# Forgetting attention by pairs of query blocks, with merged transposes and values ordered behind projections

## The chip, the cores and the metric

One core of a Trainium2 chip runs the whole kernel. The metric is the time of one execution on the device, in microseconds (us). The engines are TensorE (PE), VectorE (DVE), ScalarE (ACT), GpSimd (POOL) and SyncE (SP); each takes its own instructions in the order in which they stand in its queue. Here SP mainly issues DMAs, all transposes among them.

## The reference

A decoder trunk of two layers on 2048 tokens of 1024 channels. The even layer runs eight heads of forgetting attention (FoX) and four heads of gated linear attention (GLA) from one input projection; the odd layer runs retention and dilated attention. The change is about FoX, and about transposes that both layers share:

```python
def forgetting_attention(q, k, v, logf):
    c = jnp.cumsum(logf, axis=-1)
    ...
    def one_block(args):                       # 128 queries
        i, qi, ci = args
        s = jnp.einsum('bhqd,bhkd->bhqk', qi, k) * scale
        s = s + ci[..., :, None] - c[..., None, :]
        s = jnp.where(kpos[None, :] <= qpos[:, None], s, -jnp.inf)
        p = jax.nn.softmax(s, axis=-1)
        return jnp.einsum('bhqk,bhkd->bhqd', p, v)

def even_layer(h, norm_g, w_in, b_f, w_lr, b_lr, gla_g, w_out):
    u = rmsnorm(h, norm_g)
    z = u @ w_in
    ...                                        # FoX heads o_a, GLA heads o_b
    mix = jnp.concatenate([merge_heads(o_a), o_b], axis=-1)
    return h + (mix * jax.nn.silu(gate)) @ w_out
```

## The kernel before

Every float32 operand of a product is held as two fp16 parts, so a projection is three matmuls per tile (L163 to L165 with tokens on the rows, L173 to L175 with tokens on the columns). put_u makes the normed stream: for each of 16 row tiles it takes the sum of squares into a tile of its own (junk), splits the tile into u_hi and u_lo, and transposes each by a DMA of its own (L103) into uh and ul.

FoX goes head by head. tiles projects q, k and v of the next head, two row tiles at a time, and transposes the columns in three DMAs for every four row tiles (L413). For a query block i, scores computes the products with the keys of blocks 0 to i (L498, L499), adds the causal mask (L501), takes scores plus decay out of PSUM with their maximum in one DVE instruction per 1024 columns (L502), takes the exponential (L508), splits it into fp16 parts fx_ph (ACT, L511) and fx_pl (DVE, L512), and has SP transpose both, into fx_th (L515) and fx_tl (L516). values multiplies them with v (L524, L525) and scales the result (L526, L527, ACT L529, DVE L534); after four blocks POOL stores it to mix_d (L538).

A head's 16 blocks come in the order 12, 0, 13, 1, 14, 2, 15, 3, 8, 4, 9, 5, 10, 6, 11, 7. Each of fx_ph, fx_pl, fx_th and fx_tl has one buffer for the small blocks (under 8) and one for the large. The values of a block are emitted two steps behind its scores. merge spreads the projections for the next head (Heads.units) and those that go to memory (Extra: the gate's factors and the GLA operands, stored by POOL) evenly over these steps. Then the compile-time scheduler, with a model of time of its own, sets each engine's queue: what was emitted is where it starts from, not the order that results.

After head 6 no next head is left; the last head is merged with what is left of Extra (SHARE1), with loads of the output weights and with the first GLA rows; a rest of Extra (left, L1076) follows it. Then mix_out goes over 16 row tiles: load, gate, split into u_hi and u_lo, two transposes (yh, yl), the products, the residual, and put_u for the odd layer.

Of the kernel before, what the change touches and what calls it, by code (L numbers as in the profile page):

```python
# [29 lines left out]
SHARE2, REST2 = 80.0, 40.0  # L30
LAG = 2  # steps from scores to values
LAG_EVEN, LAG_ODD = 2, 2  # row tiles from the output's operands to its products


class Core:
    """Tools that both layers share: norms, weights in two fp16 parts, products."""

    def __init__(self, ctx, tc, cst):
# [13 lines left out]
        self.pending = None  # L52
# [8 lines left out]
    def pow2_scale(self, s, inv, ssq):  # L61
        """Powers of two s and inv = 1 / s with sqrt(ssq) * s < 2**14.5."""
# [7 lines left out]
    def rstd(self, ssq, n, shift, k=1):  # L70
        """2**shift / sqrt(ssq / n + EPS)"""
# [44 lines left out]
    def start_w(self, w, segs, gain, pool=None, space=None):  # L116
        """Columns of a weight times the gain of their rows, in two fp16 parts, and the scale's inverse."""
# [37 lines left out]
    def rows(self, out, u, t, w, c0, c1):  # L155
        """out[token, column] = u[tile t] @ w[:, c0:c1]"""
        nc = self.nc
        b, j = divmod(t, 4)
        uh, ul = u[b]
        wh, wl = w[0], w[1]  # L160
        for k in range(KT):
# [31 lines left out]
def take(units, cost):  # L193
    """The first units that come to about a cost, taken off their list."""
# [7 lines left out]
class Extra:  # L202
    """Products that go to memory: silu's two factors, and the operands of the recurrent heads."""
# [16 lines left out]
    def rows(self, n, t, k, store):  # L220
        """Row tiles t and t + 1 of 256 columns."""
# [13 lines left out]
    def cols(self, n, b, c, k, store):  # L235
        """128 columns of a block of 512 tokens."""
# [41 lines left out]
class Recurrent:  # L278
    """The steps of recurrent heads in their order, and the rows that they made."""
# [11 lines left out]
def mix_out(co, work, inputs, h_d, gate_d, gate_k, kept_d, first, ws, recur, finish, lag):  # L291
    """h + (mix * silu(gate)) @ w_out by row tiles; mix is kept_d, from column 512 * first, next to the recurrent
# [908 lines left out]
```

## Time and profile before

| what | value |
|---|---|
| three runs | 2424.91, 2433.67 (median), 2436.22 us |
| span of the profiled execution | 2434.8 us |
| PE busy | 2208.3 us (91%), clock 0.955 on the mean |
| DVE, ACT, POOL busy | 1579.2 (65%), 1166.1 (48%), 493.0 us (20%) |
| packets of transposes and stores, queue q1 | 57.2% of 16 DMA engines |

For the profiled execution only the span is recorded; it lies between the median run and the slowest one. PE is the busiest engine, so a microsecond counts where PE stands idle or has a lower clock. In the page's 40 slices of 61 us PE is at 5 to 8 tenths in the first five (up to 300 us), mostly at 8 or 9 up to about 910 us, and mostly at 9 after that. FoX runs from 170 to 1040 us, mix_out of the even layer follows to about 1310 us, then the odd layer.

### The profile page before, as it was taken

What the parts mean: (1) busy time and instruction counts of PE and PEld (TensorE: products, weight loads), DVE (VectorE), ACT (ScalarE), POOL (GpSimd) and SP (SyncE); (2) the same over time, 40 slices, a digit from 0 to 9 for tenths busy, and PEclk for the clock granted to TensorE, in tenths of its full rate; (3) what the DMA queues carried; (4) which work ended last, traced back from release to release, by engine and by line L of the source; (5) the groups of instructions that cost most, each with busy time, mean ns of one, the idle gap of its engine ahead of it and who ended that gap; (6) DMA issues with size and microseconds to landing.
All of it is one profiled execution on the core that took longest, in us unless ns stands there. A gap on an engine that the chain in (4) does not pass through costs nothing.

```text
span 2434.8 us, 52412 instructions
## 1 busy us (share of the span) xinstructions
PE 2208.3 (91%) x19956; PEld 1701.8 (70%) x19956; DVE 1579.2 (65%) x5190; ACT 1166.1 (48%) x2772; POOL 493.0 (20%) x510
## 2 busy tenths in 40 slices
PE   5877889798898899999999999999899899899998
PEld 4766768565667788764447888788787787765554
DVE  5456656765657567766557676666675666687774
ACT  5534445444545445544444555455453445633322
POOL 1020111101011111111111231222212122145341
PEclk8899889899999999999999999999999999989999
DMA  9868877878878686898876777885867768866653
GB/s 229 164 123 138 144 134 139 153 133 138 154 127 161 127 151 141 172 258 202 220 194 148 138 148 144 145 177 114 160 123 151 136 130 150 164 220 173 178 173 104
DMA packets 846652, 381.95 MB, mean 157 GB/s; under 512 B 749232, under 2 KB 805440, under 8 KB 846144
## 3 DMA queue, kind: packets, MB, share of 16 engines
q1 hardware_dynamic: 748976, 259.31, 57.2%
q0 software_dynamic: 23584, 82.33, 12.3%
q10 hardware_dynamic: 73840, 36.97, 6.5%
q8 instruction: 156, 2.56, 0.5%
q14 instruction: 96, 0.79, 0.1%
HBM read 135.40 MB, written 73.73 MB: 86 GB/s over the span
## 4 chain that ended last, share of the span: by engine, by line
PE 58%; DMA 22%; DVE 10%; issue 4%; ACT 3%; SPq 2%; POOL 1%; ACTq 0%; POOLq 0%; DVEq 0%
PE dn L163 10%; PE dn L165 10%; PE dn L164 10%; DMA fx_tl<-fx_pl 7%; PE dn L334 3%; PE dn L336 3%; PE dn L335 3%; DMA dl_pt<-dl_pl 3%; PE big L873 2%; PE big L874 2%; DMA w_raw<-in_w_in_even_dram 2%; PE aux L524 2%; PE big L498 2%; DMA fx_th<-fx_ph 1%; PE big L499 1%
## 5 line engine op out<-in xcount | busy, mean ns | idle before, releaser
L163 PE MATMUL dn<-w,uh 128*128 128x192 f16 (+1 forms) x3840 | 1012.2, 264 | 13.1 <-DVE head L407 6.7
L165 PE MATMUL dn<-w,ul 128*128 128x192 f16 (+1 forms) x3840 | 1011.1, 263 | 8.1 <-DMA ul<-u_lo 8.1
L164 PE MATMUL dn<-w,uh 128*128 128x192 f16 (+1 forms) x3840 | 1011.9, 264 | 0.0
L163 PEld LDWEIGHTS <-uh 128*128 128x128 f16 x3968 | 394.7, 100 | 51.6 <-DMA uh<-u_hi 10.9
L165 PEld LDWEIGHTS <-ul 128*128 128x128 f16 x3968 | 393.3, 100 | 42.0 <-DMA ul<-u_lo 14.4
L164 PEld LDWEIGHTS <-uh 128*128 128x128 f16 x3968 | 394.0, 100 | 32.2 <-issue 4.0
L508 ACT ACTIVATE fx_s<-fx_s,fx_nm 128x1664 f32<-128x1664 f32 (+15 forms) x128 | 153.4, 1199 | 163.0 <-DVE fx_nm L507 154.2
L880 ACT ACTIVATE dl_s<-dl_s,dl_m 128x256 f32<-128x256 f32 (+1 forms) x384 | 172.7, 452 | 114.9 <-DVE dl_m L879 99.4
L512 DVE TENSOR_TENSOR fx_pl<-fx_s,fx_ph 128x1664 f16<-128x1664 f32 (+15 forms) x128 | 165.9, 1298 | 92.4 <-ACT fx_ph L511 55.2
L876 DVE CUSTOM_DVE_ANT_0 dl_s<-big,dl_mask,hd_f 128x256 f32<-128x256 f32 (+1 forms) x384 | 141.8, 421 | 58.2 <-PE big L874 57.1
L502 DVE CUSTOM_DVE_ANT_0 fx_s<-big,cb,hd_f 128x1024 f32<-128x1024 f32 (+7 forms) x128 | 133.6, 1046 | 49.6 <-PE big L501 26.5
L511 ACT ACTIVATE fx_ph<-fx_s 128x1664 f16<-128x1664 f32 (+15 forms) x128 | 141.0, 1106 | 51.3 <-DMA fx_th<-fx_ph 45.3
L524 PE MATMUL aux<-head,fx_th 128*128 128x128 f16 x1088 | 125.8, 229 | 43.0 <-DMA fx_th<-fx_ph 41.4
L525 PE MATMUL aux<-head,fx_tl 128*128 128x64 f16 x1088 | 114.6, 201 | 45.9 <-DMA fx_tl<-fx_pl 45.7
L77 POOL TENSOR_TENSOR rs_r<-rs_v,mhalf 128x1 f32<-128x1 f32 (+2 forms) x96 | 71.1, 743 | 389.0 <-DVE rs_v L74 354.9
L883 DVE TENSOR_TENSOR dl_pl<-dl_s,dl_ph 128x512 f16<-128x512 f32 (+2 forms) x96 | 100.4, 1048 | 69.6 <-ACT dl_ph L882 38.8
L524 PEld LDWEIGHTS <-fx_th 128*128 128x128 f16 x1088 | 103.1, 104 | 54.4 <-DMA fx_th<-fx_ph 49.4
L525 PEld LDWEIGHTS <-fx_tl 128*128 128x128 f16 x1088 | 98.3, 102 | 56.7 <-DMA fx_tl<-fx_pl 54.6
L83 DVE SCALAR_TENSOR_TENSOR w<-w_raw,w_gs,w 128x256 f16<-128x256 f32 (+2 forms) x296 | 123.3, 466 | 11.0 <-ACT w L82 10.9
L873 PE MATMUL big<-head 128*128 128x256 f16 (+1 forms) x384 | 129.5, 355 | 0.6 <-DVE dl_rec L876 0.6
L874 PE MATMUL big<-head 128*128 128x256 f16 (+1 forms) x384 | 129.7, 357 | 0.0
L498 PE MATMUL big<-head 128*128 128x512 f16 (+3 forms) x320 | 114.1, 357 | 15.3 <-DVE fx_m L502 13.6
(235 smaller groups left out, 4340.1 us busy)
## 6 DMA issues: line engine op xcount, KB each, us to landing
gate_d<-x_out POOLq DMA_DIRECT2D x64, 256.0 KB, 4.0
o_gate<-gate_d SPq DMA_DIRECT2D x32, 512.0 KB, 4.6
rec_d<-dl_rec POOLq DMA_DIRECT2D x16, 528.0 KB, 5.3
dl_rec<-rec_d POOLq DMA_DIRECT2D x16, 528.0 KB, 6.2
x_h<-in_x_dram SPq DMA_DIRECT2D x16, 512.0 KB, 4.7
cb<-cum_d SPq DMA_DIRECT2D x16, 512.0 KB, 9.5
o_mix<-mix_d SPq DMA_DIRECT2D x32, 256.0 KB, 3.2
o_h<-in_x_dram SPq DMA_DIRECT2D x16, 512.0 KB, 4.6
```

The costliest lines, as they stand in the source:

```text
L163: nc.tensor.matmul(out, uh[:, k, xs], wh[:, k, c0:c1], start=k == 0, stop=False)
L164: nc.tensor.matmul(out, uh[:, k, xs], wl[:, k, c0:c1], start=False, stop=False)
L165: nc.tensor.matmul(out, ul[:, k, xs], wh[:, k, c0:c1], start=False, stop=k == KT - 1)
L498: nc.tensor.matmul(p[:, k0:k1], q, st[:, 1, ks], start=True, stop=False)
L508: nc.scalar.activation(raw[:, :n], raw[:, :n], AF.Exp, bias=nm[:, 0:1], accum_out=nm[:, 1:2])
L512: nc.vector.tensor_sub(pl[:, :n], raw[:, :n], ph[:, :n])
L524: nc.tensor.matmul(pv, th[:, k, :], v[:, k, :], start=k == 0, stop=False)
L525: nc.tensor.matmul(pv[:, 0:64], tl[:, k, :], v[:, k, 0:64], start=False, stop=k == i)
L873: nc.tensor.matmul(p[:, sp], st[:, 0, qs], st[:, 1, ks], start=True, stop=False)
L874: nc.tensor.matmul(p[:, sp], st[:, 0, qs], st[:, 2, ks], start=False, stop=True)
L876: nc.vector.tensor_tensor_reduce(out=raw[:, sp], in0=p[:, sp], in1=mask[:, 256 - 128 * len(vs):], scale=f[:, 0:1], scalar=-3.0e38, op0=OP. ...
L880: nc.scalar.activation(raw[:, sp], raw[:, sp], AF.Exp, bias=m[:, i:i + 1], accum_out=rec[:, n, 65:66])
```

## The change

Blocks go in pairs. Pair n is the blocks 15 - n and n, always 17 tiles of 128 keys (W is 17 * 128), so that a head has eight steps of one size. One copy, one subtraction, two transposes, one reciprocal and one multiplication serve both blocks; the exponential stays one per block. The scores of a pair lie in fx_s, one buffer in work for even n and one in the weights' pool for odd n (from start_gla on only the first), and the subtraction writes its fp16 result in place, into the front half of fx_s. fx_ph, fx_th and fx_tl have two buffers each. The result is scaled by one DVE instruction of 128 x 256 (o2), and two POOL additions join the parts; ACT's part of that is gone.

values is called by behind, which orders it after the last projection matmul emitted so far (co.last). periods puts LEAD1 = 4 units of Extra first in each head's period, and the last head's extra work comes in at every second place instead of every fifth. The transposes of put_u (u_x into ut), of mix_out (u_x into yt) and of q and k in the even layer (chunked, three into one) are merged; put_u's squares go to the half of u_x that later takes the low part, in place of junk.

```diff
@@ put_u
-        junk = work.tile([128, D], BF16, name="junk", bufs=1)
+        x = work.tile([128, 2, D], F16, name="u_x", bufs=U_BUFS)
         ssq = self.small.tile([128, 1], F32, name="ssq")
-        nc.scalar.activation(junk, h, AF.Square, accum_out=ssq)
-        hi = work.tile([128, D], F16, name="u_hi", bufs=U_BUFS)
-        lo = work.tile([128, D], F16, name="u_lo", bufs=U_BUFS)
+        nc.scalar.activation(x[:, 1].bitcast(BF16), h, AF.Square, accum_out=ssq)
         r = self.rstd(ssq, D, 10)
-        self.split(hi, lo, h, r[:, 0:1])
-        for part, x in zip(u[b], (hi, lo)):
-            nc.sync.dma_start_transpose(part[:, :, j * 128:(j + 1) * 128], x)
+        self.split(x[:, 0], x[:, 1], h, r[:, 0:1])
+        nc.sync.dma_start_transpose(u[b].rearrange("p s k n -> p (s k) n")[:, :, j * 128:(j + 1) * 128],
+                                    x.rearrange("p s n -> p (s n)"))
@@ mix_out
-        nc.sync.dma_start_transpose(yh, hi)
-        nc.sync.dma_start_transpose(yl, lo)
+        yt = work.tile([128, 2, KT, 128], F16, name="yt", bufs=lag + 1)
+        nc.sync.dma_start_transpose(yt.rearrange("p s k n -> p (s k) n"), x.rearrange("p s n -> p (s n)"))
@@ periods
-        both = []
+        both = [more.pop(0) for _ in range(min(lead, len(more)))]
@@ fox: scores
+    def scores(h, n):
+        st, f, cb = heads.st[h], heads.f[h], cbs[h]
+        pool = work if n % 2 == 0 or heads.wpool_closed else heads.wpool
+        raw = pool.tile([128, 2 * W], F16, name="fx_s", bufs=1)
+        x = raw.bitcast(F32)
...
+        for part, i in enumerate((15 - n, n)):
...
+                nc.vector.tensor_tensor_reduce(
+                    out=x[:, at + c * 1024:at + c * 1024 + wide], in0=p[:, :wide], in1=cb[c][:, :wide],
...
+        for part, sp in enumerate(parts):
+            nc.scalar.activation(x[:, sp], x[:, sp], AF.Exp, bias=nm[:, part:part + 1],
+                                 accum_out=nm[:, 2 + part:3 + part])
+        ph = work.tile([128, W], F16, name="fx_ph")
+        pl = raw[:, 0:W]
+        nc.scalar.activation(ph, x[:, 0:W], AF.Copy)
+        nc.vector.tensor_sub(pl, x[:, 0:W], ph)
+        th = work.tile([128, W // 128, 128], F16, name="fx_th")
+        tl = work.tile([128, W // 128, 128], F16, name="fx_tl")
+        nc.sync.dma_start_transpose(th, ph)
+        nc.sync.dma_start_transpose(tl, pl)
@@ fox: values
-        o1 = work.tile([128, 64], F32, name="fx_o1")
-        nc.scalar.activation(o1, pv[:, 0:64], AF.Copy, scale=nm[:, 3:4])
...
-        nc.vector.scalar_tensor_tensor(o[0][:, i % 4, :], pv[:, 64:128], nm[:, 3:4], o1,
-                                       op0=OP.mult, op1=OP.add)
+        nc.vector.tensor_mul(o2, pv, nm[:, 6:8, None].to_broadcast([128, 2, 128]))
...
+            nc.gpsimd.tensor_add(o[0][:, i % 4, :], o2[:, part, 0:64], o2[:, part, 64:128])
@@ fox: order
+            with co.tc.issue_after(co.last.ins):
+                values(h, n)
...
-        steps = [(0.11 * (i + 1), lambda i=i: scores(h, i), 0.086 * (i + 1), lambda i=i: values(h, i))
-                 for i in (12, 0, 13, 1, 14, 2, 15, 3, 8, 4, 9, 5, 10, 6, 11, 7)]
+        steps = [(1.9, lambda n=n: scores(h, n), 1.5, lambda n=n: behind(h, n)) for n in range(8)]
```

The rows below stand in the engines' queues as the compile-time scheduler left them: line, operation, output and inputs, size, and what it waits for by semaphore (a DMA queue as DMAHW, or an engine). The lines of the kernel before are those above; in the changed one L162 to L164 are the projections, L501, L502 and L504 the scores, L506 the reduction, L519 the subtraction, L533 and L534 the values.

On PE, at the first values of a head (block 12, then block 0), the kernel before has:

```order
L165 MATMUL dn<-w_3928,ul 128x192
L524 LDWEIGHTS fx_th_4702 [waits DMAHW4_49]
L524 MATMUL aux<-head,fx_th_4702 128x128
L498 LDWEIGHTS head
L498 MATMUL big<-head 128x256 [waits DVE_49]
L499 LDWEIGHTS head
L499 MATMUL big<-head 128x256
L501 LDWEIGHTS identb
L501 MATMUL big<-maskb,identb 128x128
L524 LDWEIGHTS fx_th_4751 [waits DMAHW5_49]
L524 MATMUL aux<-head,fx_th_4751 128x128 [waits Activation_49]
```

The changed kernel has at the first values of a head (pair 0, which holds blocks 15 and 0):

```order
L164 LDWEIGHTS ut
L164 MATMUL dn<-w_3614,ut 128x192
L533 LDWEIGHTS fx_th [waits DMAHW5_49]
L533 MATMUL aux<-head,fx_th 128x128
L534 LDWEIGHTS fx_tl [waits DMAHW6_49]
L534 MATMUL aux<-head,fx_tl 128x64
L501 LDWEIGHTS head
L501 MATMUL big<-head 128x512 [waits DVE_49]
```

The values of a large and a small block, each with its own waits, have become those of one pair, with one wait for each part right behind the last projection emitted.

On DVE, in the middle of a head, the kernel before has the subtraction of one block, the work on the next head's columns, and the reduction of the next block:

```order
L512 TENSOR_TENSOR fx_pl_6640<-fx_s_6629,fx_ph_6639 128x384 [waits DMAHW1_49,Activation_49]
L410 COPY qk_x<-qk_x 128x4x64 [waits Activation_49]
L405 SCALAR_TENSOR_TENSOR qk_x<-dn,qk_x 128x2x64 [waits PE_49,Activation_49]
L405 SCALAR_TENSOR_TENSOR qk_x<-dn,qk_x 128x2x64
L407 SCALAR_TENSOR_TENSOR head<-dn,head 128x2x64
L502 ISA fx_s_6720,fx_m<-big,cb,hd_f 128x1024 [waits PE_49]
L502 ISA fx_m 128x1
L411 COPY qk_x<-qk_x 128x4x64 [waits DVE_49]
L502 ISA fx_s_6720,fx_m<-big,cb,fx_m,hd_f 128x1024 [waits DVE_49,PE_49]
L502 ISA fx_m 128x1
```

The changed kernel has at such a place:

```order
L519 TENSOR_TENSOR fx_s<-fx_s,fx_ph 128x2176 [waits Activation_49]
L411 COPY qk_x<-qk_x 128x4x64 [waits Activation_49]
L406 SCALAR_TENSOR_TENSOR qk_x<-dn,qk_x 128x2x64 [waits PE_49,Activation_49]
L406 SCALAR_TENSOR_TENSOR qk_x<-dn,qk_x 128x2x64
L408 SCALAR_TENSOR_TENSOR head<-dn,head 128x2x64
L506 ISA fx_s,fx_m<-big,cb,hd_f 128x1024 [waits DMAHW2_49,PE_49]
L506 ISA fx_m 128x1
L412 COPY qk_x<-qk_x 128x4x64 [waits DVE_49]
L506 ISA fx_s,fx_m<-big,cb,fx_m,hd_f 128x640 [waits DVE_49,PE_49]
L506 ISA fx_m 128x1
```

The reduction now waits for a DMA too, the transpose of the pair before last, since the low parts stay in the buffer that it writes.

On PE, at the last block of the last head (block 7), the kernel before has:

```order
L165 LDWEIGHTS ul
L165 MATMUL dn<-w_64,ul 128x256
L163 LDWEIGHTS uh
L163 MATMUL dn<-w_64,uh 128x256
L164 LDWEIGHTS uh
L164 MATMUL dn<-w_64,uh 128x256
L525 LDWEIGHTS fx_tl_13997 [waits DMAHW6_49]
L525 MATMUL aux<-head,fx_tl_13997 128x64
L524 LDWEIGHTS fx_th_13996
L524 MATMUL aux<-head,fx_th_13996 128x128
```

The changed kernel has, at the last pair:

```order
L726 MATMUL big<-gl_v,gl_at 128x128 [waits DVE_49]
L728 MATMUL big<-gl_state_12154,gl_x 128x128
L726 MATMUL big<-gl_v,gl_at 128x128
L728 MATMUL big<-gl_state_12154,gl_x 128x128
L533 LDWEIGHTS fx_th [waits DMAHW7_49]
L533 MATMUL aux<-head,fx_th 128x128
L136 MATMUL aux<-w_sq,ones 128x1
L714 MATMUL aux<-ident,gl_ek 128x128 [waits DVE_49]
L733 MATMUL aux<-gl_v,gl_kd 64x128 [waits Activation_49]
L733 MATMUL aux<-gl_v,gl_kd 64x128
L534 LDWEIGHTS fx_tl [waits DMAHW0_49]
L534 MATMUL aux<-head,fx_tl 128x64
```

Projections stood between the first and the later values there, and behind them; now matmuls of GLA (L720 to L733) and of a weight's scale (L136) stand there, and no projection follows.

## Rows read from the trace of the kernel before

**Rows 1.** Windows by stage: us, busy us of each engine, clock granted, DMA share, GB/s.

```profile
0.00:160.00 160.00, 116.03 (x1256) 98.19 (x1257) 84.06 (x230) 79.60 (x141) 18.20 (x26) 0.88 0.88 178
160.00:400.00 240.00, 197.63 (x2039) 165.22 (x2039) 148.02 (x414) 118.33 (x214) 33.55 (x27) 0.90 0.80 138
400.00:900.00 500.00, 444.97 (x4494) 344.97 (x4492) 323.25 (x907) 251.61 (x462) 55.58 (x54) 0.96 0.79 142
900.00:1050.00 150.00, 143.52 (x1420) 120.33 (x1418) 101.17 (x264) 77.65 (x161) 24.72 (x32) 0.99 0.76 174
1050.00:1310.00 260.00, 252.06 (x1331) 131.47 (x1330) 163.95 (x518) 124.78 (x330) 40.19 (x62) 0.98 0.85 206
```

**Rows 2.** Waits of PE, 160 to 400 us: total us, times, longest us.

```profile
PE aux L525 <- DMA fx_tl<-fx_pl: 19.9, 9, 5.9
PE aux L524 <- DMA fx_th<-fx_ph: 19.6, 7, 6.2
```

**Rows 3.** Waits of PE, 400 to 900 us.

```profile
PE aux L524 <- DMA fx_th<-fx_ph: 21.4, 12, 3.8
PE aux L525 <- DMA fx_tl<-fx_pl: 21.4, 14, 6.1
PE big L498 <- DVE fx_m L502: 8.7, 3, 4.6
```

**Rows 4.** Waits of SP's queue, whole span.

```profile
SPq L515 <- PE aux L525: 85.0, 35, 17.4
```

**Rows 5.** Timeline of PE, 602.8 to 607.9 us: start, duration, instruction.

```profile
603.06 0.38 PE L174 MATMUL dn<-ul,w 128*128 128x512 f16 x1
603.27 0.38 PE L175 MATMUL dn<-uh,w 128*128 128x512 f16 x1
...
603.70 0.19 PE L525 MATMUL aux<-head,fx_tl 128*128 128x64 f16 x1
...
603.79 0.19 PE L525 MATMUL aux<-head,fx_tl 128*128 128x64 f16 x1
...
607.59 0.25 PE L163 MATMUL dn<-w,uh 128*128 128x192 f16 x1
607.68 0.25 PE L164 MATMUL dn<-w,uh 128*128 128x192 f16 x1
```

**Rows 6.** Groups by line and shape, whole span: busy us, mean ns, idle before.

```profile
L502 DVE CUSTOM_DVE_ANT_0 fx_s<-big,cb,hd_f 128x1024 f32<-128x1024 f32 x72 | 92.1, 1279 | 23.1 <-PE big L499 17.8 <-POOL cb L474 4.9 <-PE big L501 0.4
...
L747 POOL TENSOR_TENSOR dl_r<-dl_r,dl_r_y 128x256 f32<-128x256 f32 x64 | 51.7, 807 | 202.3 <-DVE dl_r_y L746 139.5 <-DVE w_tot L139 21.4 <-DVE w_am L133 11.0
...
L529 ACT ACTIVATE fx_o<-aux,fx_nm 128x64 f32<-128x64 f32 x128 | 37.1, 308 | 95.1 <-PE aux L525 88.8 <-PE aux L524 5.0 <-DVE w L83 0.9
...
L534 DVE SCALAR_TENSOR_TENSOR fx_o<-aux,fx_nm,fx_o 128x64 f32<-128x64 f32 x128 | 33.6, 277 | 22.7 <-ACT fx_o L529 22.5
...
L77 POOL TENSOR_TENSOR rs_r<-rs_v,mhalf 128x1 f32<-128x1 f32 x48 | 30.7, 640 | 152.1 <-DVE rs_v L74 141.0 <-DVE w_am L135 5.2 <-DVE w_am L133 4.4
...
L512 DVE TENSOR_TENSOR fx_pl<-fx_s,fx_ph 128x2048 f16<-128x2048 f32 x8 | 18.3, 2290 | 5.5 <-ACT fx_ph L511 5.5
...
L508 ACT ACTIVATE fx_s<-fx_s,fx_nm 128x2048 f32<-128x2048 f32 x8 | 16.0, 2001 | 24.1 <-DVE fx_nm L507 24.1
...
L511 ACT ACTIVATE fx_ph<-fx_s 128x2048 f16<-128x2048 f32 x8 | 15.2, 1905 | 2.2 <-DMA fx_th<-fx_ph 2.2
```

**Rows 7.** Tile fx_th, whole span: issue ns and landing us, least, median, most.

```profile
L515 SPq DMA_TRANSPOSE fx_th<-fx_ph x128: 1120/1528/6310, 165.3 to 1034.1; - x128
...
DMA to landing us min/median/max: 2.2/4.2/12.1
```

**Rows 8.** Tile fx_th, 841.85 to 841.95 us: one issue of block 15.

```profile
L515 SPq DMA_TRANSPOSE fx_th<-fx_ph x1: 1913/1913/1913, 841.9 to 841.9; - x1
...
DMA to landing us min/median/max: 4.3/4.3/4.3
```

**Rows 9.** Tile ul, 0 to 100 us: issues of put_u's second transpose.

```profile
L103 SPq DMA_TRANSPOSE ul<-u_lo x16: 1231/1922/3937, 13.8 to 94.2; - x16
```

More of the change, by code (lines that the diff above doesn't have):

```diff
@@ L30 @@
 SHARE2, REST2 = 80.0, 40.0
+W = 17 * 128
 LAG = 2
+LEAD1 = 4
 LAG_EVEN, LAG_ODD = 2, 2
@@ L51, in __init__ @@
         nc.vector.memset(self.ones, 1.0)
-        self.pending = None
+        self.pending, self.last = None, None
         self.mhalf = self.const.tile([128, 4], F32, name="mhalf")
@@ L164, in rows @@
             nc.tensor.matmul(out, uh[:, k, xs], wl[:, k, c0:c1], start=False, stop=False)
-            nc.tensor.matmul(out, ul[:, k, xs], wh[:, k, c0:c1], start=False, stop=k == KT - 1)
+            self.last = nc.tensor.matmul(out, ul[:, k, xs], wh[:, k, c0:c1], start=False, stop=k == KT - 1)
     def cols(self, out, u, b, w, c0, c1):
         nc = self.nc
-        uh, ul = u[b]
+        uh, ul = u[b][:, 0], u[b][:, 1]
         wh, wl = w[0], w[1]
@@ L174, in cols @@
             nc.tensor.matmul(out, wh[:, k, c0:c1], ul[:, k, :], start=False, stop=False)
-            nc.tensor.matmul(out, wl[:, k, c0:c1], uh[:, k, :], start=False, stop=k == KT - 1)
+            self.last = nc.tensor.matmul(out, wl[:, k, c0:c1], uh[:, k, :], start=False, stop=k == KT - 1)
 def merge(main, fill):
@@ L411, in tiles @@
             nc.vector.tensor_copy(x[:, 2, :, 64:128], x[:, 2, :, 0:64])
-            for s in range(3):
+            if self.chunked:
+                nc.sync.dma_start_transpose(
+                    self.st[h][:, t // NJ].rearrange("p s n -> p (s n)").rearrange("p (a b) -> p a b", b=128),
+                    x.rearrange("p s a b -> p (s a b)"))
+            for s in range(0 if self.chunked else 3):
                 nc.sync.dma_start_transpose(
@@ L418, in units, with periods @@
         return [(4.0, lambda t=t: self.tiles(h, t)) for t in range(0, NT, 2)]
-def periods(heads, attend, extra, first, share, rest, ready):
+def periods(heads, attend, extra, first, share, rest, ready, lead=0):
     H = 8
@@ L429, in periods @@
         more = take(extra, per - sum(c for c, _ in fill))
-        both = []
-        a, b = len(fill), len(more)
-        for n in range(a + b):
-            x = more if a * (len(both) - (a - len(fill))) < b * (a - len(fill)) and more or not fill else fill
+        both = [more.pop(0) for _ in range(min(lead, len(more)))]
+        a, b, n = len(fill), len(more), len(both)
+        for _ in range(a + b):
+            x = more if a * (len(both) - n - (a - len(fill))) < b * (a - len(fill)) and more or not fill else fill
             both.append(x.pop(0))
@@ new lines, in values @@
+    def values(h, n):
+        th, tl, nm = live.pop((h, n))
+        v = heads.v[h]
+        pv = co.ps([128, 2, 128], "aux")
+        at = 0
+        for part, i in enumerate((15 - n, n)):
+            for k in range(i + 1):
+                nc.tensor.matmul(pv[:, part, :], th[:, at, :], v[:, k, :], start=k == 0, stop=False)
+                nc.tensor.matmul(pv[:, part, 0:64], tl[:, at, :], v[:, k, 0:64], start=False, stop=k == i)
+                at += 1
+        nc.vector.reciprocal(nm[:, 4:6], nm[:, 2:4])
+        nc.vector.tensor_scalar(nm[:, 6:8], nm[:, 4:6], heads.f[h][:, 2:3], None, op0=OP.mult)
+        o2 = work.tile([128, 2, 128], F32, name="fx_o2")
+        nc.vector.tensor_mul(o2, pv, nm[:, 6:8, None].to_broadcast([128, 2, 128]))
+        for part, i in enumerate((15 - n, n)):
+            g = i // 4
+            if (h, g) not in outs:
+                outs[h, g] = [work.tile([128, 4, 64], F32, name="fx_o", bufs=3), 0]
+            o = outs[h, g]
+            nc.gpsimd.tensor_add(o[0][:, i % 4, :], o2[:, part, 0:64], o2[:, part, 64:128])
+            o[1] += 1
+            if o[1] == 4:
+                nc.gpsimd.dma_start(
+                    mix_d[g * 512:(g + 1) * 512, h * 64:(h + 1) * 64].rearrange("(j p) n -> p j n", p=128), o[0])
@@ L541, in fox, with behind @@
+    def behind(h, n):
+        if co.last is None:
+            values(h, n)
+        else:
+            with co.tc.issue_after(co.last.ins):
+                values(h, n)
     late = []
@@ L549, in attend @@
             units.insert(2 * n + 1, x)
-        behind = 2 * len(late) + 1
+        behind_late = 2 * len(late) + 1
         late[:] = wait
@@ L553, in attend @@
             for i, x in enumerate(ready):
-                units.insert(behind + 5 * i, (0.0, x))
+                units.insert(behind_late + 2 * i, (0.0, x))
             units += late
@@ L1013, in decoder @@
         wq, odd = opened("wq", 2, "right"), opened("odd", 2)
-        heads = Heads(co, (even[1], odd[1]), odd[1], wq[1], u, w_in, 0, g_even)
+        heads = Heads(co, (even[1], odd[1]), odd[1], wq[1], u, w_in, 0, g_even, True)
         extra = Extra(co, u, w_in, g_even, odd[1])
@@ L1067, in start_gla @@
             close(wq)
+            heads.wpool_closed = True
             recur.append(opened("gl", 2, "right"))
@@ L1095, in decoder @@
         pools = [even[1]]
-        heads = Heads(co, pools, pre[1], pre[1], u2, w_in_odd[0], 1024, g_odd, rope)
+        heads = Heads(co, pools, pre[1], pre[1], u2, w_in_odd[0], 1024, g_odd, False, rope)
         with tc.tile_pool(name="mo", bufs=2, reuse_waits="tile") as work:
```

103 lines of the change are left out of this document (36 added, 67 removed).

## The prediction

> **What bounds the kernel now.** I read the windows by stage first. The reader should compare PE's busy time with the length of each stage [rows 1]. The start (0 to 160 us) has 44 us without PE; heads 0 and 1 of FoX (160 to 400) have 42.4; heads 2 to 6 (400 to 900) 55.0; head 7 (900 to 1050) only 6.5, and mix_out of the even layer (1050 to 1310) 8. PE is the bound, and what a change of FoX can win is the 104 us of idle PE between 160 and 1050 us, and a little clock: 0.90 and 0.96 were granted in the two long stages, 0.99 in the full one. In the odd layer only merged transposes change beside a PE that is full, so I count nothing there.
>
> Second, the waits of PE, which say what the idle time hangs on. In heads 0 and 1 it is the landing of transposed probabilities: 19.9 and 19.6 us [rows 2]. In heads 2 to 6 it is the same, 21.4 and 21.4 us, and 8.7 us on the reduction that frees a score bank [rows 3]. That is 91 of the 97 us idle there. PE reaches the values before the probabilities have gone through exponential, copy, subtraction and transpose.
>
> Third, what holds the transposes back. SP's queue stood 85.0 us, 35 times and up to 17.4 us, on a buffer of fx_th that PE had not read to its end [rows 4]: one buffer per size serves eight blocks of a head, and SP takes its issues in order, so a late value product delays the next transpose, and that the next product.
>
> **The change, part by part: distance against chain.** A wait arises where PE has less work between a pair's last score and its first value than the chain from that score to the landed low part takes. Both can be worked out.
>
> The distance: neighbouring 512-wide matmuls start 0.21 us apart, a value pair (both parts of a tile) 0.09, 192-wide ones 0.09 [rows 5]. I counted the instructions in PE's queues. Before, head 3, a large block: 24 matmuls of 512, 18 value pairs, 10 of the next scores, 48 of 192 columns, or 5.2 + 1.5 + 1.5 + 4.0 = 12.2 us; most blocks have 12 to 19. After, head 3, pair 4: 116 of 192, 17 value pairs, 24 of 512 and some 17 score matmuls, or 9.6 + 1.5 + 5.2 + 3.0 = 19.3 us. Heads 2 to 6 lie at 19 to 29 us, head 0 at only 10.3 to 13.3, head 1 at 7.3 to 21.8.
>
> The chain for 2176 columns, scaled from the rows for 2048 and 1024 [rows 6]: the reduction of the small block 0.9, its negation 0.15; two exponentials 2176/2048 x 2.00, and 0.5 for a second start and two read-outs, 2.6 (estimates); copy 2.02; subtraction 2.43; queueing behind other work of ACT, DVE and SP 1.2 (my estimate); then the second transpose. One issue of 16 tiles took 1.91 us and landed 4.3 us after it began [rows 8]; 17 tiles give 4.6, and I take 5.2 as the median over all sizes is already 4.2 and the most 12.1 [rows 7]. The sum is 14.5 us.
>
> Heads 2 to 6: 14.5 is below 19. Two buffers of fx_th let the transpose of pair n start before the values of n - 1 are read. The 42.8 us on landings go, 10 stay for pairs whose transposes land late and for new waits of the reduction: -32. With the gaps the clock rises from 0.96 to about 0.975 over 445 us of PE work: -6. Heads 0 and 1: the distance is 2 us short in head 0 and on either side of the chain in head 1. Of 39.5 us I keep half: -20, and -5 for half the clock that 0.90 lacks against 0.95 over 198 us.
>
> The end: head 7's first five pairs have over 40 us to their values, as projections are put there. The last three have 10.2, 11.9 and 1.5 us, so they wait 4, 3 and 13 us. Before, some 115 projection matmuls (12 us) stood behind the last values and covered the first loads, gate and transpose of mix_out; now none does: +10. GLA matmuls in that gap take back 2: +28 in all. The bounds are +5, if the scheduler's gap is filled by what mix_out can start, and +45, if the one buffer of fx_s left after the pool closes makes each of these pairs wait for the one before.
>
> Off PE's path: DVE loses 128 pieces of 0.277 us and half the small operations, ACT 128 of 0.308 us [rows 6]; both have slack, so I count 0, and what they win is in the chain. POOL gains 128 additions of 128 x 64, which this trace does not show. The nearest rows are 0.640 us for one column and 0.807 for 256, so 82 to 103 us on an engine busy 114 of 890 us [rows 1, 6]. Nothing waits for them but the store, and two heads later a buffer of fx_o: 0.
>
> Transposes merged: in FoX 256 issues become 128; at the least 1.12 us each [rows 7], SP gains over 140 us of its queue, which makes the 1.2 us of queueing possible. In put_u two issues per tile, the second 1.92 us in the middle [rows 9], become one of 16 blocks, 1.91 us [rows 8]. That could give at most 16 x 1.3 = 20 us if SP were the limit of the start. Against it, the next square but one must wait for the merged transpose to land, since it writes into the same tile: a landing takes 2.4 us more than its issue [rows 8], and were that on the path at every third tile it would cost 5 x 2.4 = 12 us. DMA is at 0.88 there [rows 1], which neither changes; I take 0. In mix_out (252 of 260 us PE) one issue of 1.9 us replaces two, and its high half starts only when the low half is ready: about the same, 0, within 10 either way.
>
> The Trainium skill ("DMA: Bandwidth & Descriptors", Rules for kernel authors) says that many small transfers should be coalesced, since small ones are mostly overhead. The trace agrees in part: the smallest transposes land in 2.2 us, that of 16 tiles in 4.3 [rows 7, 8]. By the rule alone the merges of the start would give their 20 us, and the sum would be 2379 us.
>
> The sum: -20 - 5 - 32 - 6 + 28 = -35 us. Against the profiled span of 2434.8 us that is 2399.8; the median of the runs is 1.1 us below that span, so 2399 us.
>
> **The rivals.**
>
> The ring over fx_s takes the place of the waits (slower). The low part lies in fx_s until its transpose has landed, and each odd and even pair has one buffer. From the first reduction of a pair to the first of the next but one: reductions 2176/1024 x 1.279 and matmuls between them, about 4.1, and the chain 14.5, or 18.6 us. PE does 786 us of work in 64 pairs between 160 and 1050 us [rows 1], 12.3 each, 24.6 per two. So the ring decides if a landing takes over 11 us, or if SP stands as long on a buffer of fx_th, read later now as values are ordered behind projections. Landings reached 12.1 us, but the median is 4.2 [rows 7]; as DVE takes its work in order, the columns of the next head stand behind the waiting reduction. If it decides, nothing is won in heads 0 to 6 and the +28 stay: 2463 us.
>
> Everything goes (faster). With two buffers and eight equal steps all landings are covered, as 19 to 29 us suggest for most heads: 89 of 104 us of idle, 11 of clock, and the end costs 10 to 15: about 2350 us. Against it stand the short distances of heads 0 and 1 and the last three pairs.
>
> Half of it (no change). Heads 0 and 1 give nothing, since their distances are below the chain, and heads 2 to 6 half: -16 - 3 + 28 = +9, about 2443 us.
>
> The additions on POOL come late. They stand in one queue with the stores of Extra's results and the scalings of cb, which keep POOL busy in bursts. If each of 32 groups of four delays a store, and so an x_out buffer that PE's next products need, by 1 us, the forecast loses 35: 2434 us. The Trainium skill ("GPSIMD Engine Reference", 4.1 Engine selection) puts two-input elementwise work on VectorE, as GpSimd takes about twice the time. The trace agrees, 0.64 to 0.81 us around that size against 0.277 on VectorE [rows 6], but before POOL is idle for seven eighths of FoX [rows 1], so this decides only in a burst.
>
> **How the numbers follow.** Forecast 0.56, ring 0.10, everything 0.15, half 0.14, POOL late 0.05. A measurement of this kernel tells changes of more than 0.5% from none, so faster is below 2421.5 and slower above 2445.8 us. Faster: all of "everything" and nearly all of the forecast's spread (2375 to 2425), with a little of the others, 0.72. Slower: the ring, and a little of "half", 0.12. The rest, 0.16, is the same. The range leaves out the ring and the better half of "everything": 2354 to 2442 us.
>
> **What would show it.** Waits of PE on fx_th and fx_tl in heads 2 to 6 of 10 us or less in place of 42.8, and about 20 in heads 0 and 1; SP's wait on a buffer of fx_th below 30 us; PE idle in a block of some 25 us around the last three values and the first rows of mix_out. The forecast is wrong if the reductions of FoX (L506) wait on DMAs for more than 20 us in all, if landings of 17 tiles lie above 8 us in the middle, if POOL's additions hold stores up, or if the start or the odd layer differ by more than 10 us.

## The result and the profile after

The changed kernel takes 2495.18 us in the median of 4 runs (2483.73 to 2506.10), the one before 2429.29 us beside it: a ratio of 1.0272, interval 1.0230 to 1.0313. The forecast was 2399 us with a range to 2442. The profiled execution has a span of 2489.5 us. The windows by stage of the changed kernel, with the columns of [rows 1]:

```profile
0.00:160.00 160.00, 111.92 (x1191) 95.78 (x1192) 81.42 (x218) 79.49 (x138) 12.49 (x25) 0.86 0.77 170
160.00:400.00 240.00, 202.03 (x2120) 170.90 (x2119) 144.25 (x330) 108.65 (x161) 52.21 (x62) 0.92 0.78 144
400.00:900.00 500.00, 455.92 (x4682) 356.02 (x4680) 319.07 (x746) 235.83 (x365) 88.42 (x137) 0.96 0.79 147
900.00:1050.00 150.00, 132.39 (x1221) 108.42 (x1219) 83.73 (x191) 58.43 (x119) 26.44 (x38) 0.94 0.56 124
1050.00:1310.00 260.00, 213.34 (x1044) 109.32 (x1045) 140.72 (x439) 104.53 (x289) 32.96 (x52) 0.86 0.75 189
```

PE has more to do per window in heads 0 to 6 (202.0 and 455.9 us busy against 197.6 and 445.0) and far less after 900 us: 132.4 of 150 and 213.3 of 260 us, with the clock at 0.86 where it was 0.98. The waits of PE, 160 to 400 us, against [rows 2]:

```profile
PE aux L533 <- DMA fx_th<-fx_ph: 14.4, 4, 5.5
PE big L501 <- DVE fx_m L506: 8.9, 6, 6.3
PE aux L534 <- DMA fx_tl<-fx_s: 8.6, 7, 2.2
PE big L501 <- DMA head<-qk_x: 6.0, 1, 6.0
```

And from 400 to 900 us, against [rows 3]:

```profile
PE big L501 <- DMA head<-qk_x: 30.9, 5, 9.4
PE big L501 <- DVE fx_m L506: 8.4, 8, 2.9
PE aux L534 <- DMA fx_tl<-fx_s: 3.4, 3, 2.4
```

The landings of probabilities, 82.3 us before, are down to 26.4. New are 36.9 us at the first scores of six heads, which wait for the transpose of q and k. Such a wait costs more than its length: from 570 to 575 us, right behind the longest of them, PE is busy throughout at a granted clock of 0.50, the lower of its two levels (1.2 of 2.4 GHz):

```profile
570.00:575.00 5.00, 5.00 (x13) 1.83 (x14) 2.48 (x3) 0.00 (x0) 0.00 (x0) 0.50 1.32 209
```

SP's waits on a buffer of fx_th, against the 85.0 us of [rows 4], are fewer but not gone; 40.2 of these 70.4 us lie between 900 and 1060 us, in head 7:

```profile
SPq L522 <- PE aux L534: 70.4, 11, 24.4
```

From 900 to 1100 us, the end of FoX and the passage to mix_out, PE waits:

```profile
PE big L720 <- DVE o_rec L748: 13.8, 1, 13.8
PE aux L533 <- DMA fx_th<-fx_ph: 10.6, 3, 5.8
PE big L501 <- DVE fx_m L506: 5.7, 2, 5.1
PE aux L534 <- DMA fx_tl<-fx_s: 3.9, 3, 3.2
```

The 13.8 us stand at a matmul of GLA (L720), but they are not GLA's own work. PE waited for a PSUM bank that DVE frees when it scales the row before (L748), and DVE, ahead of that and of mix_out's gate (L311), stood 10.26 us on a weight of the odd layer that had not landed:

```profile
1079.55 1.75 DVE L131 TENSOR_REDUCE w_am<-w_raw 128x8 f32<-128x1536 f32 x1 [10.26 <-DMA w_raw<-in_w_in_odd_dram]
1081.63 0.88 DVE L311 SCALAR_TENSOR_TENSOR o_gate<-o_rec,gate_k,o_gate 128x256 f32<-128x256 f32 x2
1084.59 0.42 DVE L748 TENSOR_TENSOR o_rec<-big,rs_r 128x256 f32<-128x256 f32 x1
1085.16 0.80 PE L720 MATMUL big<-gl_x 64*128 64x128 f32 x4 [13.81 <-DVE o_rec L748]
```

The same instruction of DVE waits 11.6, 10.0 and 10.6 us in the traces of e1, e6 and e7 below, which leave the end as the change made it, and PE waits 13.0 to 15.0 us behind it. In e3 (more projections at the end), e4 and e5 (another spacing) PE has no wait above 6.9 us from 1000 to 1110 us.

These windows of the changed kernel show what the passage is like:

```profile
1040.00:1060.00 20.00, 10.91 (x85) 8.00 (x85) 8.76 (x19) 6.57 (x10) 1.31 (x3) 0.75 0.50 113
1060.00:1080.00 20.00, 8.23 (x58) 5.00 (x58) 6.53 (x20) 5.16 (x15) 2.11 (x4) 0.50 0.85 275
1080.00:1100.00 20.00, 12.45 (x45) 7.42 (x46) 12.86 (x44) 7.92 (x26) 2.76 (x4) 0.56 0.57 115
```

Between 1060 and 1100 us PE is busy for 8.2 and 12.5 of 20 us, and the granted clock is 0.50 and 0.56, at the lower level or near it.

To say where the time went I compare the kernels at equal PE work: every matmul counts with the distance that its shape usually has to the next start in the trace of before (the 30th percentile: 0.216 us for 512 columns, 0.082 for 192 and so on; 1980 us in all), and "lost" is the time minus that work. It is an estimate. Time lost in each part, us, worked out from the profiled execution of each kernel:

| PE work (us) | what runs there | before | changed | e1 | e2 | e3 | e4 | e5 | e9 |
|---|---|---|---|---|---|---|---|---|---|
| 0 to 50 | start, put_u | 55 | 65 | 55 | 69 | 64 | 69 | 63 | 53 |
| 50 to 700 | rest of the start, heads 0 to 6 | 159 | 123 | 140 | 147 | 144 | 122 | 128 | 136 |
| 700 to 850 | head 7 and passage | 13 | 69 | 70 | 9 | 16 | 41 | 27 | 23 |
| 850 to 1050 | mix_out, even layer | 31 | 56 | 34 | 44 | 42 | 47 | 44 | 38 |
| 1050 to 1650 | odd layer's heads | 118 | 104 | 104 | 108 | 129 | 108 | 108 | 117 |
| 1650 to 1950 | mix_out, odd layer | 70 | 84 | 62 | 76 | 78 | 87 | 79 | 70 |

The change wins 36 us in the heads, loses 10 at the start, 56 in head 7 with the passage, and 25 in mix_out; the two parts of the odd layer cancel. Together that is the 55 us between the two traces; the medians differ by 66, and the other 11 are not located.

Each column is a single execution, and those of e1 and e2 are the shortest of their runs, 14 and 9 us under the median. In the odd layer's heads, at which no edit aims, the entries go from 104 to 129, so one difference of less than some 20 us shows little. The start is firmer: 53 to 55 us in the three columns with two transposes per tile (before, e1, e9), 63 to 69 in the five with one. In e3 some 40 us of projections lie later, so its second and third rows divide at another place.

### The profile page after: what moved, and what is told of

Same layout as the page of the kernel before. It is cut to its first block, busy times and chain, and to the rows that moved or that the text cites. A ratio compares the mean times of both kernels' runs of the same rounds, so it can differ in the third digit from the quotient of the medians.

```text
span 2489.5 us, 51410 instructions
## 1 busy us (share of the span) xinstructions
PE 2231.9 (90%) x19956; PEld 1717.4 (69%) x19956; DVE 1562.9 (63%) x4870; ACT 1122.8 (45%) x2580; POOL 535.1 (21%) x638
## 5 line engine op out<-in xcount | busy, mean ns | idle before, releaser
L162 PE MATMUL dn<-w,ut 128*128 128x192 f16 (+1 forms) x3840 | 1014.4, 264 | 24.8 <-DMA ut<-u_x 10.0
L163 PE MATMUL dn<-w,ut 128*128 128x192 f16 (+1 forms) x3840 | 1013.3, 264 | 0.0
L164 PE MATMUL dn<-w,ut 128*128 128x192 f16 (+1 forms) x3840 | 1012.6, 264 | 0.0
L162 PEld LDWEIGHTS <-ut 128*128 128x128 f16 x3968 | 395.6, 100 | 65.5 <-DMA ut<-u_x 29.3
L163 PEld LDWEIGHTS <-ut 128*128 128x128 f16 x3968 | 395.0, 100 | 39.3 <-issue 10.4
L164 PEld LDWEIGHTS <-ut 128*128 128x128 f16 x3968 | 394.8, 100 | 27.3 <-issue 1.4
L506 DVE CUSTOM_DVE_ANT_0 fx_s<-big,cb,hd_f 128x1024 f32<-128x1024 f32 (+7 forms) x128 | 134.1, 1048 | 173.7 <-DMA fx_tl<-fx_s 90.3
L514 ACT ACTIVATE fx_s<-fx_s,fx_nm 128x2048 f32<-128x2048 f32 (+15 forms) x128 | 152.7, 1194 | 194.0 <-DVE fx_nm L512 193.9
L519 DVE TENSOR_TENSOR fx_s<-fx_s,fx_ph 128x2176 f16<-128x2176 f32 x64 | 155.0, 2422 | 38.4 <-ACT fx_ph L518 38.3
L501 PE MATMUL big<-head 128*128 128x512 f16 (+3 forms) x320 | 119.1, 372 | 59.9 <-DMA head<-qk_x 36.8
L533 PE MATMUL aux<-head,fx_th 128*128 128x128 f16 x1088 | 115.3, 227 | 25.0 <-DMA fx_th<-fx_ph 25.0
L85 DVE SCALAR_TENSOR_TENSOR w<-w_raw,w_gs,w 128x256 f16<-128x256 f32 (+2 forms) x296 | 123.1, 472 | 14.7 <-ACT w L84 14.5
L518 ACT ACTIVATE fx_ph<-fx_s 128x2176 f16<-128x2176 f32 x64 | 128.8, 2012 | 5.3 <-issue 3.3
L84 ACT ACTIVATE w<-w_raw,w_gs 128x256 f16<-128x256 f32 (+2 forms) x296 | 113.6, 466 | 32.8 <-DVE w_gs L143 24.0
L545 POOL TENSOR_TENSOR fx_o<-fx_o 128x64 f32<-128x64 f32 x128 | 52.9, 433 | 344.7 <-DVE fx_o L539 211.6
L534 PE MATMUL aux<-head,fx_tl 128*128 128x64 f16 x1088 | 110.1, 199 | 16.0 <-DMA fx_tl<-fx_s 15.9
```

Source lines behind the costliest of these rows:

```text
L162: nc.tensor.matmul(out, uh[:, k, xs], wh[:, k, c0:c1], start=k == 0, stop=False)
L163: nc.tensor.matmul(out, uh[:, k, xs], wl[:, k, c0:c1], start=False, stop=False)
L164: self.last = nc.tensor.matmul(out, ul[:, k, xs], wh[:, k, c0:c1], start=False, stop=k == KT - 1)
L506: nc.vector.tensor_tensor_reduce(out=x[:, at + c * 1024:at + c * 1024 + wide], in0=p[:, :wide], in1=cb[c][:, :wide], scale=f[:, 0:1], scal ...
L514: nc.scalar.activation(x[:, sp], x[:, sp], AF.Exp, bias=nm[:, part:part + 1], accum_out=nm[:, 2 + part:3 + part])
L518: nc.scalar.activation(ph, x[:, 0:W], AF.Copy)
```

## The experiments

Each ratio is to the kernel before, run on the same chip beside it. All start from the changed kernel but e2.

**e1, the merges of put_u and mix_out undone.** A small tile of the retention (rt_bs) moves to another pool to make room, here as in e6 and e8 to e12.

```diff
-        nc.sync.dma_start_transpose(u[b].rearrange(...)[:, :, j * 128:(j + 1) * 128], x.rearrange(...))
+        for part, x in zip(u[b], (hi, lo)):
+            nc.sync.dma_start_transpose(part[:, :, j * 128:(j + 1) * 128], x)
...
-        nc.sync.dma_start_transpose(yt.rearrange(...), x.rearrange(...))
+        nc.sync.dma_start_transpose(yh, hi)
+        nc.sync.dma_start_transpose(yl, lo)
```

> The changed kernel with put_u and mix_out as they were before (two transposes each, squares into a tile of their own); FoX by pairs stays. Theory A (the end of FoX has no cover, merged transposes cost little): within 10 us of the changed kernel, 2485 to 2500 us. Theory B (merged transposes are late at the start and in both mix_out stages: at equal PE work the changed kernel lost 10 us at the start and 14 us in each mix_out): 2495 - 38 = about 2457 us.

Measured: 2469.59 us, ratio 1.0140 (1.0087 to 1.0193). About half of the loss goes, nearer to theory B; the 70 us of head 7 and the passage stay, so both theories hold a part.

**e2, those merges alone in the kernel before** (the diff of e1 the other way round).

> The kernel before with the merged transposes of put_u and mix_out alone; FoX by single blocks. Theory A: within 10 us of before, 2420 to 2440 us. Theory B: 2429 + 38 = about 2467 us. If both are additive, this run and the one with FoX by pairs alone add up to the change's 66 us.

Measured: 2452.49 us, ratio 1.0087 (1.0064 to 1.0110): the merges alone cost 21 us, between the two theories. Busy time in the first 100 us, of the kernel before and then of e2:

```profile
0.00:100.00 100.00, 65.65 (x781) 53.19 (x782) 55.11 (x162) 53.36 (x102) 10.22 (x20) 0.86 1.06 219
```

```profile
0.00:100.00 100.00, 56.38 (x630) 47.53 (x631) 50.04 (x146) 49.18 (x94) 8.04 (x18) 0.84 0.97 202
```

PE gets 9 us less done with the merged transposes. ACT's waits of e2 between 10 and 110 us show at what:

```profile
ACT u_x L96 <- DMA ut<-u_x: 17.0, 8, 2.8
```

The square of a tile waits for the transpose of the tile before last, which holds both halves of its buffer; before, ACT waited 1.3 us there for a transpose (uh from u_hi).

**e6, put_u's squares in a tile of their own, transposes merged.**

```diff
-        nc.scalar.activation(x[:, 1].bitcast(BF16), h, AF.Square, accum_out=ssq)
+        junk = work.tile([128, D], BF16, name="junk", bufs=1)
+        nc.scalar.activation(junk, h, AF.Square, accum_out=ssq)
```

> The changed kernel with the merged transposes, but put_u's squares in a tile of their own as before, so that they wait for no transpose. If that wait is what the merged transposes cost, the start (10 us) and the even layer's mix_out (about 11 us) come back: 2475 us. If the merge itself costs it (the high half waits for the low one, and one long issue holds SP's queue), no change: 2490 to 2500 us.

Measured: 2492.41 us, ratio 1.0236 (1.0192 to 1.0280): no change that the intervals tell (1.0230 to 1.0313 for the changed kernel). ACT's waits, 10 to 110 us:

```profile
ACT u_x L84 <- DMA ut<-u_x: 17.1, 8, 4.3
```

The same 17 us stand one instruction later, at the high part (L84). So the wait belongs to the buffer, held until one common landing, and not to the square. That it is this wait which PE pays for is argued from the traces: no run has a third buffer, and in mix_out no wait was followed to PE.

**e3, more projections for the last head.**

```diff
-SHARE1, REST1 = 120.0, 20.0
+SHARE1, REST1 = 160.0, 20.0
```

> The changed kernel with SHARE1 = 160 in place of 120: some 40 us of projections moved from heads 0 to 6 into the last head's period, so that 20 us of them stand behind the last values. Theory A: the wait of the last pairs and the gap before mix_out shrink by some 30 us, heads 0 to 6 lose at most 10: 2470 to 2480 us. Theory B: no change at the end that matters, 2490 to 2500 us.

Measured: 2461.31 us, ratio 1.0104 (1.0056 to 1.0151). Head 7 with the passage loses 16 us in place of 69, heads 0 to 6 lose 144 in place of 123: the cover was missing at the end, and taken from the heads it is missed there. PE's waits on fx_th and fx_tl from 160 to 880 us, which both traces spend in those heads, say the same: 54.6 us in place of 26.4. Pairs 5 to 7 still share one buffer of fx_s here, as in the changed kernel, so that buffer by itself is not what the 69 us are lost to.

**e4, the last head's extra work at every fifth place.**

```diff
-                units.insert(behind_late + 2 * i, (0.0, x))
+                units.insert(behind_late + 5 * i, (0.0, x))
```

> The changed kernel with the loads and GLA starts of the last head at every fifth place as before, so that the weights' pool stays open and fx_s keeps two buffers to the end of the last head; 2 us of projections are left after the last values, GLA starts later. Theory A with the single fx_s as the cause of the last pairs' waits: their waits (some 20 us) go, but GLA's first chunks and the gap stay, 2475 us. Theory A with the missing projections as the cause: the gap stays or grows as GLA is later, 2490 to 2510 us.

Measured: 2463.18 us, ratio 1.0120 (1.0080 to 1.0161), less than either theory gave: 41 us lost at the end in place of 69, with little left after the last values. The waits of the last pairs and the empty passage would then be two costs, but this run changes three things at once, the cover, the buffer of fx_s and DVE's order in the passage, and does not part them.

**e5, at every third place**: the same line with 3.

> The changed kernel with one number changed: the last head's loads and GLA starts come in at every third place in place of every second (before: every fifth). The queues of heads 0 to 6 stay as they are; in head 7 the work from a pair's last score to its first value is 15 us or more for all pairs (2.6 to 12 for the last three in the changed kernel), and 18 us of projections stand behind the last values. If the missing cover is the cause of the 56 us that the changed kernel loses at equal work in the last head and up to mix_out, 40 to 50 us of it come back: 2495 - 45 = 2450 us. If the cause is that fx_s has one buffer at the end, little changes, 2485 us or more.

Measured: 2440.72 us, ratio 1.0027 (1.0001 to 1.0054). One number gives back 2.45% of the 2.72. Its windows at the end, and its waits of PE from 900 to 1100 us:

```profile
900.00:1050.00 150.00, 141.74 (x1322) 117.02 (x1321) 99.15 (x239) 71.62 (x146) 26.53 (x46) 0.95 0.71 176
1050.00:1310.00 260.00, 238.49 (x1202) 122.13 (x1203) 146.77 (x457) 111.89 (x299) 37.38 (x60) 0.95 0.75 190
```

```profile
PE aux L534 <- DMA fx_tl<-fx_s: 6.5, 2, 4.1
PE dn L331 <- DVE o_h L338: 3.8, 1, 3.8
PE aux L533 <- DMA fx_th<-fx_ph: 0.8, 1, 0.8
```

PE is busy 141.7 and 238.5 us in place of 132.4 and 213.3. The weights' pool closes later too, so that only pair 7 finds a single fx_s; between cover and buffer e3 decides, not this run. The 13.8 us behind the weight of the odd layer are gone too, and no run takes them out alone.

**e7, q and k in three transposes again** (the scores read the same layout).

```diff
-                nc.sync.dma_start_transpose(
-                    self.st[h][:, t // NJ].rearrange(...), x.rearrange("p s a b -> p (s a b)"))
+                for s in range(3):
+                    nc.sync.dma_start_transpose(
+                        self.st[h][:, t // NJ, s].rearrange(...), x[:, s].rearrange("p a b -> p (a b)"))
```

> The changed kernel with q, k and k's low part of the next head transposed in three DMAs again in place of one of 12 blocks; the scores read the same layout. In the changed kernel PE waits 36.8 us at the first scores of six heads for that one transpose. If the merge is the cause, some 30 us come back: 2465 us. If the cause is the load of cb that stands before it in SP's queue (9.6 to 10.3 us for an issue of usually 1.5), three small ones wait as long: 2490 to 2500 us.

Measured: 2512.07 us, ratio 1.0314 (1.0272 to 1.0357): no gain. PE's wait at the heads' first scores, 160 to 1050 us, falls from 36.8 us but stays, and its waits on the reductions and on fx_th and fx_tl grow from 58.1 to 78.1 us:

```profile
PE big L502 <- DMA head<-qk_x: 27.8, 6, 6.6
```

In the changed kernel the issues of SP around one such wait (start, duration) are:

```profile
549.33 3.36 SPq L523 DMA_TRANSPOSE fx_tl<-fx_s  x1
552.79 1.15 SPq L478 DMA_DIRECT2D cb<-cum_d  x2
554.03 9.59 SPq L414 DMA_TRANSPOSE head<-qk_x  x1
563.79 6.03 SPq L522 DMA_TRANSPOSE fx_th<-fx_ph  x1
```

The transpose of q and k, 1.46 us in the middle, takes 9.59 us behind two loads of cb. What it transposes was ready before it, and PE ran out of work later:

```profile
551.93 0.22 DVE L412 COPY qk_x<-qk_x 128x256 f16<-128x256 f16 x1
569.98 0.61 PE L501 MATMUL big<-head 128*128 128x512 f16 x1 [9.38 <-DMA head<-qk_x]
```

In all six heads that wait, q and k were ready 4.6 to 8.5 us before PE fell idle, and a landing takes 4.0 us in the middle. So late projections are not what PE waits for: in three of the six SP issues the transpose some 7 us late, behind an issue of fx_th that itself takes 7.7 to 9.1 us after a load of cb, and in the other three it lands 9.5 to 15.9 us after its issue.

**e9, as e1 and e5 together; e8, the same with three transposes of q and k.** These two are the mended change.

> FoX by pairs with all merges undone (put_u, mix_out, q and k) and the spacing of every third place. If the causes add up as I think, it keeps the 36 us that heads 0 to 6 win and loses neither the end's 45 us nor the merges' 25 to 30 us: 2495 - 45 - 27 = 2423 us, and 2395 us if the three transposes also free the starts of the heads. A rival: heads 0 to 6 win only 19 us without the merges, as in the run with them undone, so 2440 us.

> FoX by pairs, spacing of every third place, put_u and mix_out with two transposes, but q and k of the next head in one transpose (the run before this one with all merges undone had three and took 2414 us). If one transpose of 12 blocks is itself a gain, as the 17 us between the changed kernel and its version with three suggest: about 2400 us. If it makes no difference: 2414 us.

Measured: e8 2413.76 us, ratio 0.9935 (0.9890 to 0.9980); e9 2427.95 us, 0.9971 (0.9947 to 0.9995). Both are faster than before by 0.7 and 0.3%, and 2395 us is not reached. Three transposes are slower than one in the changed kernel (e7) and faster here, but the intervals overlap both times, so nothing of that size can be put down to them. Of the expectation's rival a part holds: without the merges heads 0 to 6 win about 20 us and not 36 (e1 140, e9 136; e8, worked out in the same way, 137). No run says why.

**e10, e9 with cb loaded by POOL.**

```diff
-            nc.sync.dma_start(x.rearrange("p (t i) -> p t i", i=128), src.to_broadcast([128, 8, 128]))
+            nc.gpsimd.dma_start(x.rearrange("p (t i) -> p t i", i=128), src.to_broadcast([128, 8, 128]))
```

> The same kernel with the loads of cb issued by POOL in place of SP. If the wait at the first scores of six heads (25 to 37 us in all the runs by pairs) comes from the load of cb that stands right before the transpose of q and k in SP's queue, most of it goes: 20 to 25 us less than the same kernel without this edit, about 2380 to 2390 us. If it comes from the late projections of the next head themselves, no change.

Measured: 2416.29 us, ratio 0.9944 (0.9914 to 0.9973). The wait of PE at the heads' first scores (33.5 us in e9), and the transposes of q and k (issue in ns; landing):

```profile
PE big L506 <- DMA head<-qk_x: 36.8, 6, 10.2
```

```profile
L419 SPq DMA_TRANSPOSE head<-qk_x x27: 1276/1471/5712, 161.1 to 861.7; - x27
...
DMA to landing us min/median/max: 3.6/4.3/12.5
```

The longest issue of q and k falls to 5.7 us, but landings still reach 12.5 and the waits stay. The place of cb in SP's queue is not the cause, then. The long issues still come with the loads, although these stand in POOL's queue now:

```profile
448.00 0.92 POOL L483 DMA_DIRECT2D cb<-cum_d  x1 [2.79 <-DVE fx_nm L542]
449.20 7.20 SPq L527 DMA_TRANSPOSE fx_th<-fx_ph  x1
450.44 0.89 POOL L483 DMA_DIRECT2D cb<-cum_d  x1 [1.53 <-DVE fx_m L511]
456.51 9.59 SPq L528 DMA_TRANSPOSE fx_tl<-fx_s  x1
466.20 1.45 SPq L419 DMA_TRANSPOSE head<-qk_x  x1
```

POOL begins to scale the second load at 466.32, once it has landed. That the transfers share the DMA engines would fit, but no run takes cb's transfer away, so it stays open. The 25 to 37 us of the expectation leave out e3, where the wait is 10.9 us without any edit of cb or of the transposes: 7.1 of them stand at the one head whose transpose again comes right behind two loads of cb.

**e11, e9 with the additions on DVE; e12, with both edits.**

```diff
-            nc.gpsimd.tensor_add(o[0][:, i % 4, :], o2[:, part, 0:64], o2[:, part, 64:128])
+            nc.vector.tensor_add(o[0][:, i % 4, :], o2[:, part, 0:64], o2[:, part, 64:128])
```

> The same kernel (cb on SP) with the 128 additions of the pairs' results on DVE in place of POOL. If POOL's additions are hidden, no change within 5 us, or a loss of a few us as DVE's queue gets 128 more instructions before the reductions. If POOL's queue holds stores up, 10 to 30 us faster.

> FoX by pairs, spacing of every third place, put_u and mix_out with two transposes, with both of the last two edits: cb loaded by POOL and the additions on DVE. If their gains (12 and 16 us against the same kernel without either) come from two separate causes, they add up: about 2400 us, 1.4% under the kernel before. If either came only from the scheduler's other order of the queues, the sum is smaller: 2405 to 2415 us.

Measured: e11 2411.59 us, ratio 0.9913 (0.9879 to 0.9947); e12 2417.61 us, 0.9911 (0.9880 to 0.9943). e11 touches e9's interval only at its end, so some gain is likely. PE's waits in FoX on transposes and reductions are 79 us in its trace and 90 in that of e9, each of the four groups within 6 us of the other run's, so no single wait explains it. The gains do not add up. These two have the lowest ratios of the study, 0.9% under the kernel before.

## Why the prediction was wrong, point by point

The forecast was -35 us and the traces show +55. Three terms carry the 90 us between them in like parts: the end is 28 us dearer than forecast, the merged transposes' stages (start and mix_out), counted 0, cost 35 (of which e5 gives back 12 with the end), and heads 0 to 6 win 27 less. No one of them alone would have turned the forecast's gain into a loss.

- **Landings in heads 0 to 6: right.** 30 us of waits were forecast to stay, 26.4 did, and at equal work the heads win 36 us. The forecast had 63 with the clock; it missed what comes next there, the 36.9 us at the heads' first scores. One of its signs failed: SP's wait on a buffer of fx_th was to fall below 30 us and was 70.4. And SP's queue won less than I reckoned from the shortest issue: the transposes of FoX took 509 us of it before and 438 after, 71 us less and not over 140, since an issue of 17 tiles takes 2.8 us in the middle, against 1.5 for the sizes of before. (In the distances, 9.6 us for 116 matmuls of 192 columns go by 0.082 us each and not by the 0.09 that is named; either way 19 or 20 us lie above the chain's 14.5.)
- **The end: a step that failed, by its size.** The mechanism was as described (last three pairs without cover, no projection behind), the term was +28 us with a bound of +45, and it measured 56. The pairs were not what was mis-sized: I gave their waits 20 us, and PE waited 14.5 on their landings. That leaves some 40 us (an estimate) for the passage, which I priced at 10, less 2, by the projections that had covered it. In fact the last values, 13.8 us behind DVE's wait on a weight of the odd layer, and mix_out's first rows came one after the other, and PE's clock fell to 0.50 in that stretch. e5 shows the term: one number gives back 42 of the 56 us.
- **Merged transposes: the other step that failed, 0 forecast, 21 us measured alone (e2).** I weighed the wait of the square at up to 12 us and set a gain of 20 against it. The gain was not there: the merged issue takes 2.8 us in the middle in e2's first 110 us, not the 1.91 of [rows 8], against 1.26 and 1.92 for the two before. The wait was: merged, the high half's buffer comes free only with the low half's landing, and ACT waits 17 us for that. The coalescing rule of the Trainium skill ("DMA: Bandwidth & Descriptors", Rules for kernel authors), by which the sum was 2379 us, speaks of small transfers, which it calls mostly overhead under 64 KB. Each half here is 128 x 1024 fp16, 256 KB, so the rule did not reach this merge, and no gain should have been worked out by it.
- **The ring over fx_s: there, but hidden.** DVE's waits for the low part's landing in the changed kernel:

```profile
DVE fx_s L506 <- DMA fx_tl<-fx_s: 90.3, 23, 9.7
```

- By the prediction's own sign (reductions that wait on DMAs for over 20 us) this alone said that the forecast was wrong. But of the 90.3 us on DVE at most 17.3 reach PE's score banks from 160 to 900 us (8.9 and 8.4), and before they had 8.7 from 400 us on without this ring [rows 3]. The transposes of 17 tiles (issue in ns, landing), against [rows 7]:

```profile
L522 SPq DMA_TRANSPOSE fx_th<-fx_ph x64: 2206/2762/9094, 182.3 to 1054.1; - x64
...
DMA to landing us min/median/max: 4.4/5.8/13.9
```

- The median landing is 5.8 us, near the 5.2 I took, and far from the 11 at which the ring was to decide.
- **POOL's additions** took less than the bounds of 0.64 and 0.81 us:

```profile
L545 POOL TENSOR_TENSOR fx_o<-fx_o 128x64 f32<-128x64 f32 x128 | 52.9, 433 | 344.7 <-DVE fx_o L539 211.6 <-DVE fx_nm L512 71.1 <-DVE w_tot L138 36.9
```

- The 0.277 us of VectorE in [rows 6] was another operation, which reads PSUM. The same addition on VectorE is in e11:

```profile
L550 DVE TENSOR_TENSOR fx_o<-fx_o 128x64 f32<-128x64 f32 x128 | 22.9, 220 | 0.5
```

- 0.433 us against 0.220, a factor of 2.0 (1.7 by the 0.375 us of e9). The Trainium skill ("GPSIMD Engine Reference", 4.1 Engine selection) gives about two, and the traces agree. The rival's 35 us, 1 us for each of 32 groups, should read 32. Whether the additions cost anything is the difference of e9 and e11, not settled.
- **Values ordered behind projections**, and the four units of Extra first in each period (LEAD1), were not taken out by themselves; no run here says what they are worth.

## What to carry to other kernels

Larger equal steps fill the middle of a pipeline and lengthen its end: count the cover behind the last step before and after, in the engines' queues, and price the passage to the next stage as a chain, with its clock and with every load that its engines' queues wait for. Two transfers merged into one hold both source buffers to one landing; with two buffers in the ring that can cost more than the issue saves, as the 21 us of e2 suggest. When a wait goes, look at what PE needs at the next seam (here the first scores of a head) and not only at the place that was mended.

## What was not expected of the hardware

A 12-tile transpose that issues in 1.46 us in the middle took 9.6 and 10.3 us right behind two loads of 512 KB that are spread over all partitions, and landings of such transposes still reached 12.5 us when the loads came by another engine's queue (e10). The clock that fell to its lower level in the passage is the other point: before, PE was busy 252 of 260 us there at 0.98 [rows 1], so an empty passage costs more than its idle time.
